# Two products for three: 512 and 256 moving columns in the second SwiGLU's gate and up and in the SSD output projection

## Chip, core and metric

One core of a Trainium2 chip runs the whole program. The metric is device time in microseconds (us); the kernel before takes 2457.24 us (median of 3 runs, 2456.81 to 2458.86).

## What is computed

An encoder trunk of two layers on 256 tokens plus 16 learned meta tokens (272 in all), width 2048, in fp32. Layer 0 mixes tokens with a grouped 2-D Fourier transform, layer 1 with a bidirectional Mamba-2 (SSD) mixer; each mixer is followed by a dense SwiGLU of hidden width 5632. Cut to the two places that the change touches:

```python
def swiglu_ffn(u, w_gate, w_up, w_down):
    return (jax.nn.silu(u @ w_gate) * (u @ w_up)) @ w_down

def bidir_ssd_mixer(u, w_in, ...):
    ...
    return gated_group_rms_norm(y, z, norm_w) @ w_out      # y: 272 x 4096, w_out: 4096 x 2048

for i in range(2):
    h = h + (fourier_mixer, bidir_ssd_mixer)[i](rms_norm(h, norm_mix_w[i]), ...)
    h = h + swiglu_ffn(rms_norm(h, norm_ffn_w[i]), w_gate[i], w_up[i], w_down[i])
return rms_norm(h, norm_final_w)[:, 16:]                   # the meta tokens are dropped at the end
```

Since the meta tokens are dropped, the last output projection and the last SwiGLU need only the 256 other tokens.

## The kernel before

**Split operands.** Every large product is made of fp32 numbers split in two fp32r parts, high and low. `mm3` (L102 to L106) issues three matmuls into one accumulator: high weights by high activation (L104), high weights by low activation (L105), low weights by high activation (L106). Here the weights are stationary (128 x 128, loaded anew for each matmul) and the activation moves: 272 columns where all tokens are needed, 256 where the meta tokens are not (`lo` = NM = 16). The third low-by-low product is left out everywhere.

**Weights.** `weights` (L84) takes 1 MB units by DMA on SP into three buffers; ACT casts each half to the high part `wh` (L97), DVE subtracts it from the original for the low part `wl` (L98), four buffers of each. A part is 128 x 1024 and serves 24 matmuls here (four feature blocks by two accumulators in gate and up, two feature blocks by four accumulators in the output projection).

**Products and accumulators.** `gemm_in` (L115) makes two blocks of 128 output features at a time, over 16 feature blocks `k`, alternating between two accumulators. Accumulators (`mmtile`, tag mm) are PSUM tiles of 128 x 512 fp32, four of them in rotation, so a pair can start when the pair before the last has been read out.

**Gate and up of the last SwiGLU** (`swiglu`, L360, with `lo` = 16): per pair of hidden blocks the gate product, then DVE multiplies the accumulator with 1/rms (`rbc`, L375), ACT takes the silu (L377), POOL multiplies with 1/rms once more (L378); then the up product, which DVE multiplies with that (L383), ACT rounds to `hh` (L384), POOL makes `hl` (L385). 88 such products run in all (44 blocks, gate and up), each of 16 `k`, 1408 calls of `mm3`. After each piece of the hidden layer the down product of the piece before it runs (`down1`, L787), with 512 moving columns.

**SSD output projection** (`out_group`, L557): for a group of 512 channels and a quarter `q` of the output features, two pairs (`jp`) of accumulators; a pair takes four `k` by two accumulators by `mm3`, 24 matmuls of 256 columns. DVE adds the accumulator to the residual `hT` (L567). There are eight groups, eight pairs each, 64 pairs, 512 calls of `mm3`. Groups 0 to 6 run inside the SSD stage, two steps behind the group whose inputs are computed, in between other small products of that stage (states L605 to L613, the mixing L626 to L642). The last group runs alone at the end of the stage, and each finished block of the residual there goes through `norm_block` (L142): ACT writes `gh` (L144) and a square, DVE writes `gl` (L145), POOL adds up the squares. These blocks are the operands of the first gate product.

**What sets the order.** Past the Fourier stage the program is put in order by the tile framework's scheduler, engine by engine, by its own estimates; weight parts are raised in priority (L96). Every engine then runs its list strictly in that order, and waits where an operand or a buffer isn't ready.

## Time and profile before

| | |
|---|---|
| runs | 2456.81, 2457.24, 2458.86 us; median 2457.24 |
| profiled execution, first to last instruction | 2455.8 us |
| profiled execution, own time | none is given beside its span; the median of the runs lies 1.4 us above the span |
| PE busy | 2428.0 us (99%), 17958 matmuls |
| DVE busy | 1484.5 us (60%) |
| ACT busy | 1214.1 us (49%) |
| TensorE clock granted | 0.998 of full speed |
| DMA | 438.66 MB, mean 179 GB/s |

How to read it: an engine's busy time is the union of its instructions' spans. A matmul's recorded span overlaps that of the next, so the time that a stream of them costs is the distance between starts (length of a stretch over the number of matmuls in it), not the mean duration. A wait is told with the instruction that ended it.

### The profile page before, as it was taken

The numbers are of one execution on the slowest core, as the hardware profiler recorded it, in microseconds if no ns is written. First come the engines' busy times: TensorE is split into PE (matmuls) and PEld (weight loads), VectorE is DVE, ScalarE is ACT, GpSimd is POOL, SyncE is SP. The second block draws the span as 40 slices with busy tenths as digits, with TensorE's granted clock in tenths as the row PEclk, the third lists the DMA queues.
The fourth block names the chain that finished last, engine by engine and source line by source line (L and its number), as shares of the span: only waits on it lengthen the run. The fifth ranks groups of instructions, "written<-read, shape, count | busy, mean of one in ns | idle before, by whom it ended". The sixth has DMA issues, their size and how long they took to land.

```text
span 2455.8 us, 42928 instructions
## 1 busy us (share of the span) xinstructions
PE 2428.0 (99%) x17958; PEld 2316.9 (94%) x17958; DVE 1484.5 (60%) x2020; ACT 1214.1 (49%) x1784; POOL 406.6 (17%) x361
## 2 busy tenths in 40 slices
PE   8999999999999999999999999999999999999998
PEld 8999999999999999888989989989999998989887
DVE  7564545545454568778668668668554555555556
ACT  6444333343434346878557558445444343444434
POOL 3111111010101112232221221112211010102000
PEclk9999999999999999999999999999999999999999
DMA  5555555555555555655455555454555555555553
GB/s 164 175 178 179 173 173 176 181 175 172 175 181 177 172 173 175 213 175 186 164 179 193 177 172 184 159 172 157 201 187 178 189 189 189 189 190 188 189 192 134
DMA packets 115506, 438.66 MB, mean 179 GB/s; under 512 B 7360, under 2 KB 8080, under 8 KB 115136
## 3 DMA queue, kind: packets, MB, share of 16 engines
q1 hardware_dynamic: 110336, 417.86, 50.4%
q0 software_dynamic: 4832, 17.99, 2.3%
q8 instruction: 141, 2.31, 0.4%
q14 instruction: 53, 0.43, 0.0%
q10 hardware_dynamic: 144, 0.07, 0.0%
HBM read 433.66 MB, written 2.23 MB: 177 GB/s over the span
## 4 chain that ended last, share of the span: by engine, by line
PE 89%; DVE 3%; DMA 3%; issue 2%; ACT 2%; POOL 1%; SPq 0%; DVEq 0%; ACTq 0%; POOLq 0%
PE mm L105 29%; PE mm L106 28%; PE mm L104 28%; DMA pb<-scr 2%; DVE wl L98 1%; PE tp L642 1%; ACT wh L97 1%; DVE ca L544 1%; PE tp L626 0%; PE tp L665 0%; DMA w<-fnet_w_out 0%; POOL pb L701 0%; ACT pb L584 0%; DMA x<-x 0%; PE tp L608 0%
## 5 line engine op out<-in xcount | busy, mean ns | idle before, releaser
L98 DVE TENSOR_TENSOR wl<-w,wh 128x1024 fp32r<-128x1024 f32 x786 | 970.0, 1236 | 840.7 <-ACT wh L97 832.7
L97 ACT CAST wh<-w 128x1024 fp32r<-128x1024 f32 x786 | 822.8, 1048 | 1096.6 <-PE mm L105 809.2
L105 PE MATMUL mm<-gl,wh 128*128 128x272 f32 (+2 forms) x3600 | 1026.0, 285 | 0.0
L106 PE MATMUL mm<-gh,wl 128*128 128x272 f32 (+2 forms) x3600 | 1022.3, 284 | 0.5 <-DVE wl L98 0.5
L104 PE MATMUL mm<-gh,wh 128*128 128x272 f32 (+2 forms) x3600 | 1022.4, 284 | 0.1
L104 PEld LDWEIGHTS mm<-gh,wh 128*128 128x128 f32 x3600 | 678.2, 188 | 1.1 <-issue 0.5
L106 PEld LDWEIGHTS mm<-gh,wl 128*128 128x128 f32 x3600 | 676.3, 188 | 0.9 <-DVE wl L98 0.7
L105 PEld LDWEIGHTS mm<-gl,wh 128*128 128x128 f32 x3600 | 676.1, 188 | 0.8 <-issue 0.5
L378 POOL TENSOR_TENSOR s<-s,rbc 128x272 f32<-128x272 f32 (+1 forms) x88 | 96.4, 1113 | 816.4 <-ACT s L377 816.4
L105 PE MATMUL mm<-hl,wh 128*128 128x272 f32 x704 | 203.7, 289 | 0.0
L106 PE MATMUL mm<-hh,wl 128*128 128x272 f32 x704 | 202.7, 288 | 0.0
L104 PE MATMUL mm<-hh,wh 128*128 128x272 f32 x704 | 200.9, 285 | 0.0
L385 POOL TENSOR_TENSOR hl<-t,hh 128x272 fp32r<-128x272 f32 (+1 forms) x88 | 97.0, 1121 | 397.1 <-ACT hh L384 397.1
L104 PE MATMUL mm<-yh,wh 128*128 128x256 f32 x512 | 146.5, 288 | 3.8 <-DVE hT L567 3.3
L105 PE MATMUL mm<-yl,wh 128*128 128x256 f32 x512 | 143.6, 281 | 0.5 <-DVE yl L671 0.5
L106 PE MATMUL mm<-yh,wl 128*128 128x256 f32 x512 | 143.5, 281 | 0.0
L105 PE MATMUL mm<-wl,hh 128*128 128x512 f32 x352 | 137.1, 390 | 0.0
L104 PE MATMUL mm<-wh,hh 128*128 128x512 f32 x352 | 137.0, 389 | 0.0
L106 PE MATMUL mm<-wh,hl 128*128 128x512 f32 x352 | 137.0, 389 | 0.0
L104 PEld LDWEIGHTS mm<-hh,wh 128*128 128x128 f32 x704 | 132.9, 189 | 0.0
L106 PEld LDWEIGHTS mm<-hh,wl 128*128 128x128 f32 x704 | 132.3, 188 | 0.0
L105 PEld LDWEIGHTS mm<-hl,wh 128*128 128x128 f32 x704 | 132.1, 188 | 0.0
(279 smaller groups left out, 2858.5 us busy)
## 6 DMA issues: line engine op xcount, KB each, us to landing
w<-ffn_w_gate SPq DMA_DIRECT2D x88, 1024.0 KB, 5.1
w<-ffn_w_up SPq DMA_DIRECT2D x88, 1024.0 KB, 5.1
w<-w_down SPq DMA_DIRECT2D x80, 1024.0 KB, 5.1
w<-w_xbc SPq DMA_DIRECT2D x48, 1024.0 KB, 5.2
w<-w_z SPq DMA_DIRECT2D x32, 1024.0 KB, 5.3
w<-ssd_w_out SPq DMA_DIRECT2D x32, 1024.0 KB, 5.1
w<-fnet_w_out SPq DMA_DIRECT2D x16, 1024.0 KB, 5.1
pb<-scr POOLq DMA_DIRECT2D x32, 512.0 KB, 5.6
```

What stands on the lines that cost most here:

```text
L97: SC.copy(wh, w[:, ks, :])
L98: V.tensor_tensor(out=wl, in0=w[:, ks, :], in1=wh.bitcast(F32), op=ALU.subtract)
L104: PE.matmul(ps, lhs[0], rhs[0], start=start, stop=False)
L105: PE.matmul(ps, lhs[0], rhs[1], start=False, stop=False)
L106: PE.matmul(ps, lhs[1], rhs[0], start=False, stop=stop)
L378: GP.tensor_tensor(out=s1, in0=s1, in1=rbc[:, lo:], op=ALU.mult)
L385: GP.tensor_tensor(out=hl[:, f, :], in0=t2, in1=hh[:, f, :].bitcast(F32), op=ALU.subtract)
L544: V.scalar_tensor_tensor(out=a[:, o0:o1], in0=u[:, i0 : i0 + o1 - o0], scalar=w(j), in1=a[:, o0:o1], op0=ALU.mult, op1=ALU.add)
L642: PE.matmul(py[:, e * HD : (e + 1) * HD], kern[c][:, e, :], xt[:, c, e * HD : (e + 1) * HD], start=True, stop=True)
```

## The change

The high and the low part of the moving activation stand next to each other for each feature block, 256 + 256 columns. `mm3t` takes the place of `mm3` in the two places: one matmul of the high weights over all 512 columns, which leaves high-by-high in the first half of the accumulator and high-by-low in the second; then one of the low weights over the first 256 columns, added to the first half. The halves are added when the accumulator is read: in the SwiGLU ACT copies the second half to SBUF and DVE adds the first (`halves`), then the old multiplication follows from SBUF; in the output projection DVE adds both halves to the residual one after the other. For this `gh` and `gl` become two views of one buffer `g2`, and `gt`, a third view that lies over them, holds the pairs for the last SwiGLU; `yh` and `yl` become halves of one tile `yt`. The second matmul closes the accumulation. (The diff also drops comments, which is left out here.)

```diff
-    gh = const.tile([P, NB, L], F32R, name="gh")
-    gl = const.tile([P, NB, L], F32R, name="gl")
+    g2 = const.tile([P, 2 * NB * L], F32R, name="g2")
+    gh, gl = (g2[:, i * NB * L : (i + 1) * NB * L].rearrange("p (b t) -> p b t", t=L) for i in range(2))
+
+    gt = g2[:, : NB * 2 * S].rearrange("p (b t) -> p b t", t=2 * S)
...
+    def mm3t(ps, lhs, twin, start, stop):
+
+        PE.matmul(ps, lhs[0], twin, start=start, stop=False)
+        PE.matmul(ps[:, :S], lhs[1], twin[:, :S], start=False, stop=stop)
+
+    def halves(out, ps):
+        SC.copy(out, ps[:, S:])
+        V.tensor_tensor(out=out, in0=ps[:, :S], in1=out, op=ALU.add)
...
                 for j in range(2):
-                    mm3(pss[j][:, :n], wsl(u, k, j * P), gsl(k0 + k, lo), k0 + k == 0, k0 + k == NB - 1)
+                    if lo == NM:
+                        mm3t(pss[j], wsl(u, k, j * P), gt[:, k0 + k, :], k0 + k == 0, k0 + k == NB - 1)
+                    else:
+                        mm3(pss[j][:, :n], wsl(u, k, j * P), gsl(k0 + k, lo), k0 + k == 0, k0 + k == NB - 1)
...
-        SC.activation(gh[:, b, lo:], hT[:, b, lo:], AF.Identity, bias=0.0, scale=wcol)
-        V.scalar_tensor_tensor(out=gl[:, b, lo:], in0=hT[:, b, lo:], scalar=wcol,
-                               in1=gh[:, b, lo:].bitcast(F32), op0=ALU.mult, op1=ALU.subtract)
+
+        high, low = (gt[:, b, :S], gt[:, b, S:]) if lo == NM else gsl(b, lo)
+        SC.activation(high, hT[:, b, lo:], AF.Identity, bias=0.0, scale=wcol)
+        V.scalar_tensor_tensor(out=low, in0=hT[:, b, lo:], scalar=wcol,
+                               in1=high.bitcast(F32), op0=ALU.mult, op1=ALU.subtract)
...
-                    V.tensor_tensor(out=t1, in0=ps[:, :n], in1=rbc[:, lo:], op=ALU.mult)
+                    if lo == NM:
+                        halves(t1, ps)
+                    V.tensor_tensor(out=t1, in0=t1 if lo == NM else ps[:, :n], in1=rbc[:, lo:], op=ALU.mult)
...
-                    V.tensor_tensor(out=t2, in0=ps[:, :n], in1=s2[j], op=ALU.mult)
+                    if lo == NM:
+                        halves(t2, ps)
+                    V.tensor_tensor(out=t2, in0=t2 if lo == NM else ps[:, :n], in1=s2[j], op=ALU.mult)
...
-                        mm3(pss[j][:, :S], wsl(u, k, (2 * jp + j) * P), (yh[:, k, :], yl[:, k, :]), k == 0, k == 3)
+                        mm3t(pss[j], wsl(u, k, (2 * jp + j) * P), yt[:, k, :], k == 0, k == 3)
...
-                    V.tensor_tensor(out=hT[:, m, NM:], in0=ps[:, :S], in1=hT[:, m, NM:], op=ALU.add)
+                    for half in (ps[:, :S], ps[:, S:]):
+                        V.tensor_tensor(out=hT[:, m, NM:], in0=half, in1=hT[:, m, NM:], op=ALU.add)
...
-            yh = sp.tile([P, 4, S], F32R, tag="yh", name="yh", bufs=2)
-            yl = sp.tile([P, 4, S], F32R, tag="yl", name="yl", bufs=2)
+            yt = sp.tile([P, 4, 2 * S], F32R, tag="yt", name="yt", bufs=2)
+            yh, yl = yt[:, :, :S], yt[:, :, S:]
```

The scheduler places the new instructions, and moves others. Up to the first output projection the lists of all engines are the same but for names. Three places follow; a name's number tells its buffer apart, and the new program numbers its lines and buffers anew (L587 there is L567 here, L100 is L98, L691 is L671, L160 is L145, L631 is L611).

DVE in the first out group (channels group 0): pairs of accumulators mm_12510/12511, mm_12538/12539, mm_12576/12577 before. Before:

```order
L567 TENSOR_TENSOR hT_69<-mm_12510,hT_69 128x256
L567 TENSOR_TENSOR hT_69<-mm_12511,hT_69 128x256
L671 SCALAR_TENSOR_TENSOR yl_11525<-tp_12435,cols_74,yh_11524 128x128
L671 SCALAR_TENSOR_TENSOR yl_11525<-tp_12448,cols_74,yh_11524 128x128
L567 TENSOR_TENSOR hT_69<-mm_12538,hT_69 128x256
L671 SCALAR_TENSOR_TENSOR yl_11525<-tp_12435,cols_74,yh_11524 128x128
L671 SCALAR_TENSOR_TENSOR yl_11525<-tp_12448,cols_74,yh_11524 128x128
L567 TENSOR_TENSOR hT_69<-mm_12539,hT_69 128x256
L98 TENSOR_TENSOR wl_12663<-w_12660,wh_12662 128x1024
L98 TENSOR_TENSOR wl_12667<-w_12660,wh_12666 128x1024
L567 TENSOR_TENSOR hT_69<-mm_12576,hT_69 128x256
```

Now, from the second pair (mm_12528/12529) on, with the third (mm_12560/12561) and fourth (mm_12582/12583):

```order
L587 TENSOR_TENSOR hT_69<-mm_12528,hT_69 128x256
L100 TENSOR_TENSOR wl_12635<-w_12632,wh_12634 128x1024
L587 TENSOR_TENSOR hT_69<-mm_12528,hT_69 128x256
L100 TENSOR_TENSOR wl_12639<-w_12632,wh_12638 128x1024
L587 TENSOR_TENSOR hT_69<-mm_12529,hT_69 128x256
L587 TENSOR_TENSOR hT_69<-mm_12560,hT_69 128x256
L587 TENSOR_TENSOR hT_69<-mm_12529,hT_69 128x256
L587 TENSOR_TENSOR hT_69<-mm_12560,hT_69 128x256
L587 TENSOR_TENSOR hT_69<-mm_12561,hT_69 128x256
L587 TENSOR_TENSOR hT_69<-mm_12582,hT_69 128x256
L587 TENSOR_TENSOR hT_69<-mm_12561,hT_69 128x256
```

Each accumulator is now read twice. The two weight parts come between the reads of the second pair, and the second read of mm_12529 stands behind the first read of mm_12560, an accumulator that PE finishes later.

PE at the fourth pair of the same group. Before, its matmuls alternated between the two accumulators and the state products (L605 to L613) stood behind the pair. Now:

```order
L117 MATMUL mm_12582<-yt_10956,wl_12553 128x256
L116 MATMUL mm_12582<-yt_10956,wh_12556 128x512
L117 MATMUL mm_12582<-yt_10956,wl_12557 128x256
L116 MATMUL mm_12582<-yt_10956,wh_12556 128x512
L117 MATMUL mm_12582<-yt_10956,wl_12557 128x256
L628 MATMUL tp_12607<-xw_12458,btok_11558 128x512
L116 MATMUL mm_12583<-yt_10956,wh_12552 128x512
L117 MATMUL mm_12583<-yt_10956,wl_12553 128x256
```

The first accumulator is completed, then a state product, then the second is begun. A group's first state product (xwM) moves up in the same way, ahead of the third pair.

DVE in the last out group, four of whose pairs are mm_17826/17827, mm_17858/17859, mm_17900/17901 and mm_17932/17933. Before (pairs mm_18183/18184, mm_18221/18222, mm_18269/18270), the reads stood two by two:

```order
L567 TENSOR_TENSOR hT_69<-mm_18183,hT_69 128x256
L567 TENSOR_TENSOR hT_69<-mm_18184,hT_69 128x256
L145 SCALAR_TENSOR_TENSOR gl_71<-hT_69,cols_74,gh_70 128x256 x2
L567 TENSOR_TENSOR hT_69<-mm_18221,hT_69 128x256
L567 TENSOR_TENSOR hT_69<-mm_18222,hT_69 128x256
L98 TENSOR_TENSOR wl_18348<-w_18345,wh_18347 128x1024
L145 SCALAR_TENSOR_TENSOR gl_71<-hT_69,cols_74,gh_70 128x256 x2
L567 TENSOR_TENSOR hT_69<-mm_18269,hT_69 128x256
L98 TENSOR_TENSOR wl_18352<-w_18345,wh_18351 128x1024
```

Now:

```order
L587 TENSOR_TENSOR hT_69<-mm_17858,hT_69 128x256
L160 SCALAR_TENSOR_TENSOR g2_70<-hT_69,cols_73,g2_70 128x256
L100 TENSOR_TENSOR wl_17967<-w_17964,wh_17966 128x1024
L160 SCALAR_TENSOR_TENSOR g2_70<-hT_69,cols_73,g2_70 128x256
L587 TENSOR_TENSOR hT_69<-mm_17858,hT_69 128x256
L100 TENSOR_TENSOR wl_17971<-w_17964,wh_17970 128x1024
L160 SCALAR_TENSOR_TENSOR g2_70<-hT_69,cols_73,g2_70 128x256
L587 TENSOR_TENSOR hT_69<-mm_17859,hT_69 128x256
L587 TENSOR_TENSOR hT_69<-mm_17900,hT_69 128x256
L587 TENSOR_TENSOR hT_69<-mm_17859,hT_69 128x256
```

The reads of a pair are spread: two weight parts and three low parts of the norm stand between the first and the last read of mm_17858/17859.

## Rows read from the trace of the kernel before

**Rows 1.** The page: engines' busy time, the granted clock in 40 slices, the chain.
```profile
PE 2428.0 (99%) x17958; PEld 2316.9 (94%) x17958; DVE 1484.5 (60%) x2020; ACT 1214.1 (49%) x1784; POOL 406.6 (17%) x361
...
PEclk9999999999999999999999999999999999999999
...
PE 89%; DVE 3%; DMA 3%; issue 2%; ACT 2%; POOL 1%; SPq 0%; DVEq 0%; ACTq 0%; POOLq 0%
```

**Rows 2.** Busy time by stretch: gate and up, down, z, five out stretches.
```profile
core 0: us, PE busy (x) PEld busy (x) DVE busy (x) ACT busy (x) POOL busy (x), PEclk, DMA share, GB/s
1934.00:2023.84 89.84, 89.84 (x769) 89.84 (x768) 45.68 (x49) 37.99 (x46) 15.19 (x14) 1.00 0.57 189
2023.85:2067.40 43.55, 43.55 (x194) 36.05 (x193) 24.08 (x25) 17.48 (x18) 2.18 (x2) 1.00 0.56 192
1137.56:1159.87 22.31, 22.31 (x99) 18.09 (x97) 17.72 (x22) 19.80 (x33) 0.91 (x1) 1.00 0.55 195
1652.68:1664.11 11.43, 11.43 (x98) 11.43 (x98) 7.12 (x13) 3.67 (x5) 2.33 (x2) 1.00 0.41 132
1162.24:1176.24 14.00, 14.00 (x105) 12.40 (x104) 11.12 (x21) 11.29 (x22) 6.71 (x6) 1.00 0.57 202
1176.25:1190.25 14.00, 14.00 (x108) 12.80 (x106) 7.91 (x14) 4.79 (x5) 1.16 (x1) 1.00 0.46 153
1680.52:1706.31 25.79, 23.80 (x192) 23.01 (x193) 22.16 (x40) 17.39 (x37) 11.90 (x11) 1.00 0.37 127
```

**Rows 3.** Timeline of PE where the down product ends and gate begins: start, duration.
```profile
2067.19 0.39 PE L106 MATMUL mm<-wh,hl 128*128 128x512 f32 x1
2067.41 0.28 PE L104 MATMUL mm<-gh,wh 128*128 128x256 f32 x1
2067.53 0.28 PE L105 MATMUL mm<-gl,wh 128*128 128x256 f32 x1
```

**Rows 4.** Groups by shape, PE: line, operation, shapes, count | busy us, mean ns.
```profile
L104 PE MATMUL mm<-gh,wh 128*128 128x256 f32 x1408 | 394.5, 280 | 0.1
...
L104 PE MATMUL mm<-yh,wh 128*128 128x256 f32 x512 | 146.5, 288 | 3.8 <-DVE hT L567 3.3 <-ACT yh L670 0.5
```

**Rows 5.** Groups by shape, DVE and ACT: the operations nearest to the added ones.
```profile
L567 DVE TENSOR_TENSOR hT<-mm,hT 128x256 f32<-128x256 f32 x128 | 48.9, 416 | 9.2 <-PE mm L106 9.1
...
L383 DVE TENSOR_TENSOR t<-mm,s 128x256 f32<-128x256 f32 x44 | 17.1, 425 | 7.0 <-PE mm L106 6.1 <-POOL s L378 0.9
```

**Rows 6.** Groups by shape, ACT: a copy of 256 columns from PSUM.
```profile
L554 ACT COPY xt<-tp 128x256 f32<-128x256 f32 x32 | 11.6, 362 | 0.2 <-PE tp L553 0.2
```

**Rows 7.** Timeline of the first out group from 1162.24: DVE's reads, PE's state product.
```profile
1165.99 0.74 DVE L567 TENSOR_TENSOR hT<-mm,hT 128x256 f32<-128x256 f32 x2
1166.66 0.59 DVE L671 SCALAR_TENSOR_TENSOR yl<-tp,cols,yh 128x128 fp32r<-128x128 f32 x2
...
1173.78 1.12 PE L605 MATMUL tp<-xwM,btokM 16*128 16x512 f32 x2
```

**Rows 8.** Waits of PE from 1000 to 1706: us in total, times, longest.
```profile
PE mm L104 <- DVE hT L567: 3.3, 4, 1.6
```

**Rows 9.** Groups of DVE from 1680.5 to 1713.3, the last out group and its tail.
```profile
L98 DVE TENSOR_TENSOR wl<-w,wh 128x1024 fp32r<-128x1024 f32 x10 | 12.2, 1216 | 1.3 <-ACT wh L97 1.2
L145 DVE SCALAR_TENSOR_TENSOR gl<-hT,cols,gh 128x256 fp32r<-128x256 f32 x16 | 10.9, 702 | 0.9 <-ACT gh L144 0.9
L567 DVE TENSOR_TENSOR hT<-mm,hT 128x256 f32<-128x256 f32 x16 | 6.1, 413 | 0.7 <-PE mm L106 0.6
L671 DVE SCALAR_TENSOR_TENSOR yl<-tp,cols,yh 128x128 fp32r<-128x128 f32 x7 | 2.2, 345 | 0.8 <-ACT yh L670 0.8
```

**Rows 10.** Timeline of DVE after the last out group: last add, last low part.
```profile
1710.87 0.41 DVE L567 TENSOR_TENSOR hT<-mm,hT 128x256 f32<-128x256 f32 x1
...
1712.34 0.95 DVE L145 SCALAR_TENSOR_TENSOR gl<-hT,cols,gh 128x256 fp32r<-128x256 f32 x1
```

More of the change, by code (lines that the diff above doesn't have):

```diff
@@ L555, in to_tokens, with out_group @@
             SC.copy(dstM, ps[:NM, 2 * P : 3 * P])
-        def out_group(gi, q, yh, yl):
+        def out_group(gi, q, yt):
             u = weights(w_out, gi * 4, 4, q * 512, 512)
@@ L683, in group_rest @@
             later(4, norm)
-            return yh, yl
+            return yt
         def decays(gi):
@@ L764, in encoder @@
                         for q in (2 * h2, 2 * h2 + 1):
-                            out_group(go, q, *outs[go])
+                            out_group(go, q, outs[go])
                             if go == G - 2 and h2 == 1:
@@ L772, in encoder @@
         for q in range(4):
-            out_group(G - 1, q, *outs[G - 1])
+            out_group(G - 1, q, outs[G - 1])
     with ExitStack() as fx:
```

## The prediction, as made before the changed kernel ran

> **What bounds the kernel now.** I read the page first: PE is busy 99% of the span at full granted clock in all 40 slices, and 89% of the chain that ended last is PE [rows 1]. So time is won only where PE issues less or faster, and lost where PE is made to wait. Second, busy time by stretch, to get PE's price for a matmul: a stream of matmuls costs the distance between starts, so a stretch's length over its count. Gate and up of the last SwiGLU: 768 matmuls of 256 columns start in 89.84 us, 117.0 ns each. The down product: 192 of 512 columns in 43.55 us, 226.8 ns. The z product of the SSD stage, also 512 columns: 96 in 22.31 us, 232.4 ns. An undisturbed half group of the output projection: 96 of 256 columns in 11.43 us, 119.1 ns, the first start included [rows 2]. The timeline shows the same step by step where 512 columns give way to 256: 0.22, then 0.12 us [rows 3]. Third, the waits: over the SSD stage PE's largest wait for DVE's residual adds is 3.3 us in four times [rows 8], and nearly all of what its matmuls waited for in the out groups is that add [rows 4]. DVE is the second engine to watch: 45.68 of 89.84 us in gate and up, but 11.12 of 14.00 us in the first half of an out group, and 22.16 of 25.79 in the last group [rows 2].
>
> **The part that is removed.** A call of `mm3` was three matmuls of 256 columns, now it is one of 512 and one of 256: the same 768 columns, one weight load and one start fewer. By the distances: gate and up 3 x 117.0 = 351.0 ns before; out groups 3 x 119.1 = 357.3. Afterwards one 512 and one 256. No row shows the two in turn, so I bound the pair. The dear end is 232.4 + 119.1 = 351.5, with the z row; the cheap end 226.8 + 113.4 = 340.2, if the 256 columns go at the down product's price per column (half of 226.8). I take 226.8 + 119.1 = 345.9: the down product is nearest, because its moving and stationary operands lie in the same even steps as those of `gt` and `yt` with the weight parts do, while in z the stationary part steps by 272 columns; and 119.1 is the even-step price of 256 columns. That gives, with 1408 calls in gate and up and 448 in out groups 0 to 6 [rows 4]:
>
> - gate and up: 1408 x (351.0 - 345.9) = 1408 x 5.1 ns = 7.2 us (ends: 0.7 lost, 15.2 won);
> - out groups 0 to 6: 448 x (357.3 - 345.9) = 448 x 11.4 ns = 5.1 us (ends: 2.6 and 7.7).
>
> So 12.3 us less (ends 1.9 and 22.9). The last group's 64 calls are left out here, since DVE sets its pace (below).
>
> From 226.8 and 119.1 the rows make a start cost 11.4 ns beside its columns (2 x 119.1 - 226.8). The Trainium skill (TensorE: Matmul & The Clock Gate, Back-to-back issue gap) gives a matmul of N columns N / 2.4 + 2.5 ns at full clock; by it a start fewer saves 2.5 ns, and 1856 calls save an estimated 4.6 us, which speaks against most of this gain. By it the two prices would be an estimated 216 and 109 ns; the trace has 226.8 and 117.0 to 119.1, so the two differ, and the sum goes by the rows.
>
> **What is added in gate and up: nothing on the path.** 88 ACT copies at about 0.36 us [rows 6] and 88 DVE adds at about 0.42 us [rows 5], with the old multiplication reading SBUF. A pair of products lasts 32 calls x 0.346 = 11.1 us on PE; in this time DVE gets 2 x 0.42 = 0.85 us and ACT 0.72 us more. DVE there is half idle, ACT more so [rows 2]. The accumulators of a pair are wanted again a whole pair later, 11.1 us, and the copy, the add and the multiplication take under 3 us. Without that cover it would be 88 x 0.8 = 70 us, so it's the four accumulators that carry it. The first pair even frees its accumulators sooner than before, as the add needs no 1/rms. At the end of the kernel the last piece's `hh` and `hl` come about 0.8 us later; the down product of the piece before them, 48 matmuls at 226.8 ns or 10.9 us, runs meanwhile.
>
> **What is added in out groups 0 to 6.** 16 DVE adds of 0.416 us more in each [rows 5], 6.7 us in some 28 us, where DVE is busy 11.12 + 7.91 us of 28.00 [rows 2]: room overall, 25.7 of 28, but the first half comes to 11.12 + 3.33 = 14.45 us in a half that PE would pass in 13.6 (14.00 less 32 x 11.4 ns). Behind an add wait the next weight parts on DVE, and for the add waits the pair after the next, whose accumulators it frees. I walked through the first group along the new order, with the durations of the rows. Pair 1 starts at 1162.24 and a pair lasts 8 x 0.346 = 2.77 us. The reads of pair 1 start at 1165.99, as now; four adds and two `yl` in between end near 1168.1. Pair 3 starts at 1167.8 plus the state product that now stands ahead of it, 1.12 us [rows 7]: no wait. Pair 2's first accumulator is free near 1170.6, behind one weight part of 1.2 us [rows 9]; its second near 1173.0, behind the second weight part and the first read of pair 3. Pair 4 begins with the first accumulator at 1171.7, and the state product fills the time up to the second: no wait either. The moved state products thus absorb the delay. I put 2 us on all seven groups, for the one in which DVE was already late (the longest wait of 1.6 us [rows 8]) and small rests elsewhere; ends 0 and 17 us.
>
> **What is added in the last out group.** From 1680.5 to 1713.3 DVE did 12.2 + 10.9 + 6.1 + 2.2 = 31.4 us of work in 32.8 us [rows 9]. Sixteen more adds at 0.413 are 6.6 us, 38.0 in all, so this work ends 5.2 us later than now, near 1718 instead of 1713.3 [rows 10]. PE's own work would be shorter, but its pairs wait for accumulators, and the weight parts for the next stage (ten in the stretch) stand in the same list. Walking the order as above, PE starts the gate product some 5 us later than at 1706.3. I take 5 us; ends 2 (weight parts get ahead of the reads in time) and 7.
>
> **Sum.** -12.3 + 2 + 5 = -5.3 us against the profiled execution, whose span is 2455.8: 2450.5. The median of the runs lies 1.4 us above that span, so I forecast **2451.9 us**. 0.2% is 4.9 us: about what a measurement of this kernel can tell from no change; faster means under 2452.3, slower over 2462.2.
>
> **Rivals.**
>
> 1. *All adds are covered.* Then 12.3 us and the last group's own 64 x 11.4 ns = 0.7 are won: 2457.2 - 13.0 = 2444.2. For it: PE waited so little for DVE until now [rows 8]. Against: DVE has 1.4 us left in the last group's 32.8 [rows 9]. 0.17.
> 2. *Time goes with the columns alone.* The 512-column matmul then takes the z stretch's 232.4 ns in company with the 256: gate and up lose 0.7, out groups win 2.6, and with the 2 + 5 of waits the time is 2457.2 - 1.9 + 7 = 2462.3, at the edge of slower. For it: 512 columns did take 232.4 where the product stood in the SSD stage [rows 2], and the first distance after a change of size is not settled. Against: 44 us of down product at 226.8. 0.20. By the 2.5 ns a start of the Trainium skill (same page and section) the time would be an estimated 2457.2 - 4.6 + 7 = 2459.6.
> 3. *DVE sets the pace of every out group.* A pair's two accumulators are free 0.83 us later each time; if that reaches PE in three pairs of each of the seven groups, 7 x 3 x 0.8 = 16.8 us instead of 2: 2457.2 - 12.3 + 16.8 + 5 = 2466.7, slower. It decides where the last of a pair's four adds ends after the start of the pair after the next. For it: the second read of a pair now stands behind a read that waits for a later pair, and DVE has 14.45 us of work in a half of 13.6. Against: the walk above finds the state products in the right places. 0.18.
>
> **How the numbers follow.** The forecast has 0.45, its own range 2446 to 2458 by the pair's price (2 ns a call is 3.7 us) and 2 to 3 us on the last group. Range over the cases: from 2441, which holds rival 1 and a cheaper pair, to 2464, which holds rival 2; most of rival 3 is left out. Faster: rival 1 and six tenths of the forecast, 0.44. Slower: nearly all of rival 3 and under half of rival 2, 0.24. Same: 0.32.
>
> **What would show it.** In gate and up, pairs of starts of about 227 and 119 ns, so a piece of eight blocks in 88.5 us instead of 89.84; 233 and 119 there is rival 2. PE's waits for `hT` are 2 us or less before the last group and 4 to 6 us in it, with the first gate matmul about 5 us later relative to the group's start; waits of 2 us in each group are rival 3, none in the last group rival 1. DVE x216 and ACT x88 more, PE x1920 fewer. I'd be wrong altogether if the 512 and 256 in turn cost under 340 or over 352 ns, or if PE waited in gate and up.

## The result and the profile after

| | before | after |
|---|---|---|
| median of the runs | 2457.02 us (2455.92 to 2458.86, 4 runs) | 2475.2 us (2474.3 to 2478.73, 4 runs) |
| profiled execution, first to last instruction | 2455.8 us | 2473.3 us (its own time 2475.11) |
| ratio of the runs | | 1.0076, 95% interval 1.0064 to 1.0088 |

The change makes the kernel 18.7 us slower (0.0076 x 2457; interval 15.7 to 21.6). Below, a ratio is turned into us over the kernel before in the same way, since every batch of runs had runs of the kernel before beside it. The forecast was 2451.9 us, its range ended at 2464: the time lies outside, and the sign is wrong.

The page of the kernel after answers to [rows 1]: 1920 matmuls fewer, 216 DVE and 88 ACT instructions more, as foreseen, but PE is busy for 2.6 us more, and its share of the chain fell from 89% to 84%.

```profile
PE 2430.6 (98%) x16038; PEld 2233.0 (90%) x16038; DVE 1563.5 (63%) x2236; ACT 1236.3 (50%) x1872; POOL 415.1 (17%) x361
...
PE 84%; DVE 6%; issue 3%; ACT 3%; DMA 3%; POOL 1%; SPq 0%; DVEq 0%; ACTq 0%; POOLq 0%
```

Where the time went is read by stretch. I cut both executions at the same three matmuls: the first of out group 0, the first of out group 5 (from there groups 5 to 7 follow one another), and gate's first. The kernel before, in the columns of [rows 2]:

```profile
1162.24:1623.49 461.25, 457.73 (x3179) 418.29 (x3178) 329.09 (x530) 286.34 (x499) 88.20 (x71) 1.00 0.52 177
1623.49:1706.31 82.82, 80.37 (x639) 76.10 (x638) 63.94 (x120) 39.75 (x70) 20.33 (x18) 1.00 0.41 142
```

The kernel after: a piece of eight blocks in gate and up, the down product behind it, then the same two stretches, and three places inside the second of them.

```profile
1950.98:2040.85 89.87, 89.87 (x513) 78.77 (x512) 51.87 (x62) 41.88 (x61) 18.37 (x14) 1.00 0.56 189
2040.85:2084.41 43.56, 43.56 (x195) 36.05 (x193) 25.04 (x27) 17.91 (x20) 2.67 (x2) 1.00 0.56 190
1162.38:1629.90 467.52, 459.86 (x2859) 403.48 (x2858) 354.48 (x610) 284.17 (x499) 80.15 (x71) 1.00 0.51 174
1629.90:1723.21 93.31, 81.79 (x447) 67.78 (x446) 80.01 (x167) 40.24 (x71) 17.70 (x18) 0.98 0.39 133
1684.60:1689.42 4.82, 0.00 (x1) 0.00 (x1) 4.77 (x16) 1.03 (x1) 0.00 (x0) 1.00 0.62 210
1689.42:1692.48 3.06, 3.06 (x15) 3.06 (x16) 0.41 (x2) 0.73 (x2) 0.00 (x0) 0.56 0.74 238
1693.87:1723.21 29.34, 23.69 (x128) 19.62 (x129) 26.22 (x51) 17.01 (x36) 9.98 (x11) 1.00 0.29 98
```

Three things are to be seen. Gate and up gained nothing: 89.87 us for the piece that took 89.84 [rows 2], so 89.87 / 256 = 351.0 ns a pair. The stretch of groups 0 to 4, with the products between them, is 6.3 us longer, and the stretch of groups 5 to 7 is 10.5 us longer. Inside this last one stand 4.82 us in which PE starts nothing while DVE is busy for 4.77, then 3.06 us at a granted clock of 0.56 (mostly the 1.2 GHz level), and a last group of 29.34 us instead of 25.79 [rows 2]. From gate's first matmul to the last matmul both kernels take 738.1 us.

The waits of PE over the SSD stage answer to [rows 8]. The adds' 3.3 us became 8.6 (2.9 in group 3, 5.6 in the last group), and there is a new wait of 4.8 us, for `dg`, which no add writes:

```profile
PE mm L116 <- DVE hT L587: 8.6, 6, 2.9
PE tp L685 <- DVE dg L680: 4.8, 1, 4.8
PE mm L107 <- DVE wl L100: 2.6, 3, 1.4
PE mm L116 <- DVE yt L691: 1.0, 1, 1.0
PE tp L570 <- DVE yt L691: 0.8, 2, 0.5
PE tp L625 <- POOL xwM L621: 0.7, 1, 0.7
PE tp L570 <- ACT xs L565: 0.5, 1, 0.5
```

`dg` is the diagonal of 1/rms by which a group's gated output is scaled on its way back to feature-major. In the last group it ends a row of twelve DVE operations on two columns (`sums`, then the eleven of `rsqrt`). DVE's timeline of the kernel before, from `sums` to `dg`, takes 5.3 us, with four adds and two weight parts in between:

```profile
1671.32 0.17 DVE L654 TENSOR_SCALAR sums<-sums 128x2 f32<-128x2 f32 x1 [0.52 <-ACT sqj L647]
...
1672.39 0.74 DVE L567 TENSOR_TENSOR hT<-mm,hT 128x256 f32<-128x256 f32 x2
...
1676.65 0.43 DVE L660 TENSOR_TENSOR dg<-ident,rgy 128x256 f32<-128x256 f32 x1
```

In the kernel after it takes 8.4 us, with nine adds and four weight parts:

```profile
1680.58 0.17 DVE L674 TENSOR_SCALAR sums<-sums 128x2 f32<-128x2 f32 x1 [0.51 <-ACT sqj L667]
1680.65 1.22 DVE L100 TENSOR_TENSOR wl<-w,wh 128x1024 fp32r<-128x1024 f32 x1
1681.79 0.42 DVE L587 TENSOR_TENSOR hT<-mm,hT 128x256 f32<-128x256 f32 x1
...
1684.53 0.15 DVE L151 SCALAR_TENSOR_TENSOR rgy<-rgt,rgy 128x2 f32<-128x2 f32 x1
1684.60 0.42 DVE L587 TENSOR_TENSOR hT<-mm,hT 128x256 f32<-128x256 f32 x1
1684.93 0.15 DVE L149 TENSOR_TENSOR rgt<-rgy 128x2 f32<-128x2 f32 x1
...
1687.82 1.22 DVE L100 TENSOR_TENSOR wl<-w,wh 128x1024 fp32r<-128x1024 f32 x1
1688.95 0.42 DVE L680 TENSOR_TENSOR dg<-ident,rgy 128x256 f32<-128x256 f32 x1
```

An add stands between almost every two operations of the chain, and DVE idles nowhere in it. PE's timeline shows what waits: group 6's last matmul starts at 1684.33, and the next thing in PE's order needs `dg`.

```profile
1684.33 0.28 PE L117 MATMUL mm<-yt,wl 128*128 128x256 f32 x1
1689.42 3.48 PE L685 MATMUL tp<-dg,yg 128*128 128x128 f32 x16 [4.82 <-DVE dg L680]
1693.87 0.50 PE L116 MATMUL mm<-yt,wh 128*128 128x512 f32 x1 [0.97 <-DVE yt L691]
```

Before, `dg` was ready near 1677.1 and PE came for it at 1678.1: one microsecond of slack. The stage ahead had shifted by 6.4 us, but `dg` came 12.3 us later (1676.65 to 1688.95): 2.9 us because `sums` came later still, 3.0 us because the chain got longer. The row of operations ahead of `sums`, the last group's second mixing, got longer in the same way. From its first operation on DVE to `sums` it took 5.6 us, with two adds and one weight part in between, and takes 10.6 us, with eleven adds and two weight parts. Its start before and after:

```profile
1665.72 0.68 DVE L627 TENSOR_TENSOR yg<-tp,tm 128x512 f32<-128x512 f32 x1
1670.02 0.69 DVE L647 TENSOR_TENSOR yg<-tp,tm 128x512 f32<-128x512 f32 x1
```

From group 6's first matmul to the last group's, the kernel before takes 27.84 us and the kernel after 34.62, so 6.8 more: the wait of 4.8, 1.4 for the products with `dg` at the lower clock (3.06 us instead of 1.67), and 0.5 in the wait for `yt` behind them.

```profile
1652.68:1680.52 27.84, 27.38 (x228) 26.71 (x228) 21.33 (x46) 10.22 (x15) 2.33 (x2) 1.00 0.44 152
1659.25:1693.87 34.62, 28.84 (x164) 24.97 (x163) 28.22 (x68) 11.28 (x18) 2.34 (x2) 0.95 0.45 152
```

### The profile page after: what moved, and what is told of

It is laid out like the page before. It is cut to its first block, busy times and chain, and to the rows that moved or that the text cites. A ratio compares the mean times of both kernels' runs of the same rounds, so it can differ in the third digit from the quotient of the medians.

```text
span 2473.3 us, 39469 instructions
## 1 busy us (share of the span) xinstructions
PE 2430.6 (98%) x16038; PEld 2233.0 (90%) x16038; DVE 1563.5 (63%) x2236; ACT 1236.3 (50%) x1872; POOL 415.1 (17%) x361
## 4 chain that ended last, share of the span: by engine, by line
PE 84%; DVE 6%; issue 3%; ACT 3%; DMA 3%; POOL 1%; SPq 0%; DVEq 0%; ACTq 0%; POOLq 0%
PE mm L107 18%; PE mm L108 18%; PE mm L106 18%; PE mm L116 17%; PE mm L117 9%; DMA pb<-scr 2%; DVE wl L100 2%; DVE ca L563 1%; ACT wh L99 1%; ACT pb L604 1%; PE tp L662 1%; DMA w<-fnet_w_out 0%; PE tp L646 0%; DVE pb L606 0%; DVE hT L587 0%
## 5 line engine op out<-in xcount | busy, mean ns | idle before, releaser
L100 DVE TENSOR_TENSOR wl<-w,wh 128x1024 fp32r<-128x1024 f32 x786 | 973.3, 1241 | 759.7 <-ACT wh L99 757.4
L107 PE MATMUL mm<-g,wh 128*128 128x272 f32 (+1 forms) x2192 | 633.7, 289 | 0.0
L108 PE MATMUL mm<-g,wl 128*128 128x272 f32 (+1 forms) x2192 | 630.8, 288 | 0.5 <-DVE wl L100 0.5
L106 PE MATMUL mm<-g,wh 128*128 128x272 f32 (+1 forms) x2192 | 628.2, 287 | 0.0
L116 PE MATMUL mm<-g,wh 128*128 128x512 f32 x1408 | 494.7, 394 | 0.0
L106 PEld LDWEIGHTS mm<-g,wh 128*128 128x128 f32 x2192 | 414.0, 189 | 0.6 <-issue 0.2
L108 PEld LDWEIGHTS mm<-g,wl 128*128 128x128 f32 x2192 | 411.9, 188 | 0.9 <-DVE wl L100 0.7
L107 PEld LDWEIGHTS mm<-g,wh 128*128 128x128 f32 x2192 | 411.8, 188 | 0.5 <-issue 0.5
L117 PE MATMUL mm<-g,wl 128*128 128x256 f32 x1408 | 398.2, 283 | 0.0
L116 PEld LDWEIGHTS mm<-g,wh 128*128 128x128 f32 x1408 | 264.5, 188 | 60.9
L117 PEld LDWEIGHTS mm<-g,wl 128*128 128x128 f32 x1408 | 265.0, 188 | 0.2
L395 POOL TENSOR_TENSOR s<-s,rbc 128x272 f32<-128x272 f32 (+1 forms) x88 | 105.3, 1206 | 808.6 <-ACT s L394 808.6
L116 PE MATMUL mm<-yt,wh 128*128 128x512 f32 x512 | 189.5, 412 | 9.9 <-DVE hT L587 8.6
L404 POOL TENSOR_TENSOR hl<-t,hh 128x272 fp32r<-128x272 f32 (+1 forms) x88 | 107.4, 1230 | 388.5 <-ACT hh L403 388.5
L117 PE MATMUL mm<-yt,wl 128*128 128x256 f32 x512 | 142.1, 282 | 0.0
```

What stands on the lines that cost most here:

```text
L100: V.tensor_tensor(out=wl, in0=w[:, ks, :], in1=wh.bitcast(F32), op=ALU.subtract)
L106: PE.matmul(ps, lhs[0], rhs[0], start=start, stop=False)
L107: PE.matmul(ps, lhs[0], rhs[1], start=False, stop=False)
L108: PE.matmul(ps, lhs[1], rhs[0], start=False, stop=stop)
L116: PE.matmul(ps, lhs[0], twin, start=start, stop=False)
L117: PE.matmul(ps[:, :S], lhs[1], twin[:, :S], start=False, stop=stop)
```

## The experiments

Theory A, formed from these rows: the pair of 512 and 256 costs what the three matmuls of 256 cost, so there is nothing to win, and all of the loss comes from the added `hT` adds in the SSD stage, a large part of it from group 6's, which hold up the last group's norm. The rivals are told with each run.

**Each half of the change alone.** First gate and up changed, the output projection as before:

```diff
-                        mm3t(pss[j], wsl(u, k, (2 * jp + j) * P), yt[:, k, :], k == 0, k == 3)
+                        mm3(pss[j][:, :S], wsl(u, k, (2 * jp + j) * P), (yt[:, k, :S], yt[:, k, S:]), k == 0, k == 3)
...
-                    for half in (ps[:, :S], ps[:, S:]):
+                    for half in (ps[:, :S],):
```

> Only the second SwiGLU's gate and up have the matmul of 512 columns and their halves added; the SSD output projection is as before. Theory A (the time of a pair goes with its 768 columns, 351.6 ns in the trace after against 351.2 ns for the three before, and the whole loss lies ahead of gate and up): within 1.5 us of the kernel before, say 0 to +1.5. Rival B (the pair does save 5 ns of 351, and the trace after hides it behind something that the output projection leaves behind): 1408 pairs give 7 us, so -7. Rival C (the loss is that of gate and up, the shift ahead of them only a delay that would be caught up): about +17.

Measured: 1.0002 (0.9992 to 1.0011), +0.5 us. A and not B: no gain was hidden. Then the output projection alone, where gate and up keep `mm3` and read the accumulator as before:

```diff
-                    if lo == NM:
+                    if False:
                         mm3t(pss[j], wsl(u, k, j * P), gt[:, k0 + k, :], k0 + k == 0, k0 + k == NB - 1)
...
```

> Only the SSD output projection has the matmul of 512 columns and two adds a block; gate and up are as before. Theory A: the whole loss is here, +16 to +18.5 over the kernel before, and the start of gate stands 16.8 us later as in the trace after. Rival C: within 2 us of the kernel before. Either way the sum of this and of the run with gate and up alone tells whether the two halves of the change touch each other: theory A has them add up to +18 within 1.5 us.

Measured: 1.0072 (1.0059 to 1.0085), +17.7 us. The two add up to 18.2 of the 18.7 us. Within the intervals they do not touch each other, and the loss is the output projection's.

**The adds or the form of the matmuls.** The output projection alone again. Once with the pair, but a single add:

```diff
-                    for half in (ps[:, :S], ps[:, S:]):
+                    for half in (ps[:, :S],):
```

> Gate and up as before; in all eight SSD output groups the matmuls of 512 and 256 columns as changed, but one hT add a block instead of two: the high-low products are summed and left out of the result. Theory A (the adds and the place they take in VectorE's order are what costs; the pair itself costs what the three matmuls cost): -1 to +4 over the kernel before, the wait for dg under 1 us, the waits for hT in the last group under 2 us in sum. Rival F (the form of the matmuls costs, by state products that now stand inside pairs and by longer waits for an accumulator of 512 columns): +10 or more.

And once with two adds, but matmuls of the old size:

```diff
-                        mm3t(pss[j], wsl(u, k, (2 * jp + j) * P), yt[:, k, :], k == 0, k == 3)
+                        w = wsl(u, k, (2 * jp + j) * P)
+                        PE.matmul(pss[j][:, :S], w[0], yt[:, k, :S], start=k == 0, stop=False)
+                        PE.matmul(pss[j][:, S:], w[0], yt[:, k, S:], start=False, stop=False)
+                        PE.matmul(pss[j][:, :S], w[1], yt[:, k, :S], start=False, stop=k == 3)
```

> Gate and up as before; in all eight SSD output groups three matmuls of 256 columns as before the change, but the high-low one into the other half of the accumulator, so that two hT adds a block are needed as in the change. Theory A: the loss is there with matmuls of the old size, +13 to +19 over the kernel before, with a wait of 3 to 5 us for dg. Rival F: within 4 us of the kernel before.

Measured: one add 1.0011 (1.0002 to 1.0020), +2.7 us; two adds with old matmuls 1.0054 (1.0040 to 1.0067), +13.3 us. With one add, by stretch:

```profile
1163.09:1625.34 462.25, 457.98 (x2859) 402.22 (x2858) 328.18 (x530) 285.91 (x499) 86.64 (x71) 1.00 0.51 176
1625.34:1708.07 82.73, 79.64 (x447) 66.47 (x446) 64.84 (x121) 39.93 (x72) 18.72 (x18) 1.00 0.42 146
```

With two adds and matmuls of 256 columns:

```profile
1163.38:1629.09 465.71, 460.76 (x3180) 420.50 (x3178) 354.23 (x610) 285.14 (x499) 86.89 (x71) 0.99 0.52 175
1629.09:1723.89 94.80, 85.23 (x640) 80.25 (x638) 78.39 (x166) 41.69 (x72) 20.94 (x19) 0.95 0.37 123
```

The stretch of groups 5 to 7 has its old length with one add (82.73 against 82.82) and is 12 us longer with two, though the matmuls have the old size. (The profiled execution with two adds is the slowest of its five, 2475.14 us against a median of 2472.3, and its granted clock in this stretch is 0.95; the median is 13.3 us over the kernel before.) The wait for `dg` is there in the second and not in the first:

```profile
PE tp L688 <- DVE dg L683: 4.4, 1, 4.4
```

So A against F for the larger part of the loss. It is not shown that the form costs nothing: by the runs it is worth 2.7 us with one add and 4.4 with two (17.7 less 13.3), both with intervals that begin near nothing. In the stretches it shows as 1.0 us in groups 0 to 4 with one add; two executions of one and the same order, those of the kernel before and of gate and up alone, differ there by 1.4 us (461.25 and 459.83).

**Which group's adds.** The whole change, with only the last group's output projection put back, and then with those of groups 6 and 7 (`gi >= G - 2` in its place):

```diff
-                        mm3t(pss[j], wsl(u, k, (2 * jp + j) * P), yt[:, k, :], k == 0, k == 3)
+                        if gi == G - 1:
+                            mm3(pss[j][:, :S], wsl(u, k, (2 * jp + j) * P), (yt[:, k, :S], yt[:, k, S:]), k == 0, k == 3)
+                        else:
+                            mm3t(pss[j], wsl(u, k, (2 * jp + j) * P), yt[:, k, :], k == 0, k == 3)
...
-                    for half in (ps[:, :S], ps[:, S:]):
+                    for half in (ps[:, :S], ps[:, S:])[: 1 if gi == G - 1 else 2]:
```

> The changed kernel, with the last SSD group's output projection done as before, in three matmuls of 256 and one add a block; groups 0 to 6 are as changed. Theory A (the last group's own double adds cost some 4.7 us in waits of TensorE for hT, while the wait for dg comes from group 6's adds and stays): 4 to 6 us faster than the changed kernel, the wait for dg still 3 to 5 us. Rival D (VectorE's whole load around the last group sets it): over 9 us faster, and the wait for dg gone too. Rival E (the waits for hT before the last group's end were hidden ones, the last group being bound by its weights' parts): within 2 us of the changed kernel.

> The changed kernel, with the output projection of groups 6 and 7 in three matmuls of 256 and one add a block as before, groups 0 to 5 as changed. Theory A (the wait of 4.8 us for dg and the low clock behind it come from group 6's second adds, which stand ahead of the norm's small operations; the waits for hT from group 7's): the stretch from group 6 to gate is back at its length before, and what is left over the kernel before is +6 to +9, from groups 0 to 5. Rival M (the wait for dg comes from what groups 0 to 5 left behind, such as a later mixing): the wait for dg is still over 3 us and the time +11 to +13.

Measured: without the last group 1.0053 (1.0041 to 1.0066), +13.0 us, so its part of the change is worth 5.6 us, and the wait for `dg` stays:

```profile
PE tp L688 <- DVE dg L683: 4.8, 1, 4.8
PE mm L116 <- DVE hT L590: 2.9, 1, 2.9
```

Without groups 6 and 7: 1.0016 (1.0007 to 1.0025), +3.9 us. The wait for `dg` is gone, and the stretch of groups 5 to 7 is back near its length before, 82.98 us against 82.82:

```profile
1161.40:1625.26 463.86, 459.14 (x2860) 403.55 (x2858) 355.32 (x610) 283.96 (x499) 81.04 (x71) 1.00 0.50 175
1625.26:1708.24 82.98, 80.45 (x575) 72.92 (x574) 69.96 (x136) 39.66 (x70) 19.62 (x18) 1.00 0.41 141
```

Group 6's part of the change is thus worth 9.1 us (13.0 - 3.9, numbers with intervals of 3 and 2 us to either side), though no matmul of group 6 waits for an add. The run puts back its second adds and its form together; that the wait for `dg` comes with the adds and not with the form is what the runs with one add and with two show. Group 6's own stretch holds 6.7 of the 9.1 us: it takes 34.53 us without the last group's part and 27.84, as before, without both. Another 2.7 us lie far ahead of it, from group 0 to group 1 (85.94 and 83.29 us), where both programs have the same order on every engine; why the one execution was slower there is not shown. What is left for groups 0 to 5, with gate and up, is 3.9 us, less than the 6 to 9 expected: in that number A was too high, since it rested on the 6.3 us that groups 0 to 4 lost in the kernel after.

**Only the order of the chain.** The whole change, with the last group's norm ahead of its time in DVE's list:

```diff
-            later(3, lambda: mix(1))
+            def mix1():
+                with tc.high_priority(offset=300) if gi == G - 1 else ExitStack():
+                    mix(1)
+
+            later(3, mix1)
...
-            later(4, norm)
+            later(3 if gi == G - 1 else 4, norm)
```

(and the same priority around `sums`, `rsqrt` and `dg`.)

> The changed kernel, with the last SSD group's second mixing and the small operations of its norm (rsqrt and the diagonal) put ahead of the hT adds of group 6 in VectorE's order, and nothing else; the number of adds is the same. Theory A (the norm's chain of 14 small operations waits in VectorE's queue behind adds that wait for TensorE's last products of group 6, so that TensorE finds nothing to do for 4.8 us and its clock is 0.56 in the 3 us after): 5 to 8 us faster than the changed kernel, that is +10 to +13 over the kernel before, no wait of over 1.5 us for dg, granted clock 1.00 there. Rival D (the adds themselves keep VectorE too busy, so that what the chain gains the adds lose, and the wait moves to hT): within 2 us of the changed kernel.

Measured: 1.0061 (1.0048 to 1.0073), +15.0 us, so 3.7 us faster than the changed kernel: less than the 5 to 8 expected, more than D's 2, though the two intervals overlap. The wait for `dg` is gone and the clock 1.00, and the stretch is 4.0 us shorter (89.31 against 93.31), but it holds a new wait, and the adds of the last group wait as before:

```profile
PE mm L116 <- DVE hT L587: 6.0, 6, 1.6
PE mm L116 <- DVE rgt L149: 2.2, 1, 2.2
```

In the order that came out, ten adds still alternate with the chain; it is the four weight parts that moved away. From group 5's first matmul to the last group's it takes 58.9 us, against 64.0 in the changed kernel and 57.0 before, so the order alone gives back 5.1 of 6.9 us there. The wait of 2.2 us is one of group 6's products, and the last group takes 1.1 us more than in the changed kernel. D has this much for it: DVE is busy for the same 80 us of groups 5 to 7 (80.06 and 80.01; 63.94 before), and no run shows an order that mends all of the loss. The trace also corrects a point of the expectation: the chain did not stand behind adds that wait for PE, since DVE idled nowhere; it stood behind adds and weight parts that take DVE's time.

**The price of the pair.** Why 351 ns, when 226.8 + 119.1 was to be had from the rows? The timeline of the kernel after, where the down product ends and gate begins, answers to [rows 3]:

```profile
2084.18 0.39 PE L108 MATMUL mm<-wh,hl 128*128 128x512 f32 x1
2084.41 0.40 PE L116 MATMUL mm<-g,wh 128*128 128x512 f32 x1
2084.64 0.27 PE L117 MATMUL mm<-g,wl 128*128 128x256 f32 x1
2084.75 0.39 PE L116 MATMUL mm<-g,wh 128*128 128x512 f32 x1
```

From start to start a 512 takes 0.23 us and a 256 some 0.12; over the trace from 1800 to 2100 the means are 230.8 and 120.3 ns. Eight runs bear on this. First the 512 by itself, in the kernel with gate and up alone changed:

```diff
-                        mm3t(pss[j], wsl(u, k, j * P), gt[:, k0 + k, :], k0 + k == 0, k0 + k == NB - 1)
+                        PE.matmul(pss[j], wsl(u, k, j * P)[0], gt[:, k0 + k, :], start=k0 + k == 0, stop=k0 + k == NB - 1)
```

> As the run with gate and up alone changed, without the matmul of 256 columns (the product of the weights' low parts with the activation's high ones is left out in gate and up). Prices the 512 by itself: theory A: 229 to 233 ns from start to start, as in the z products, which makes 1408 x (351 - 231) = 169 us less than before, some 2288 us. Rival G (the 512 alone is cheaper, 216 to 227 ns): 2267 to 2283 us.

Measured: 2294.36 us, 0.9334 (0.9317 to 0.9351), 6 us more than A's total. The piece of eight blocks:

```profile
1874.44:1934.16 59.72, 59.72 (x257) 48.06 (x256) 49.29 (x61) 41.13 (x60) 17.03 (x14) 1.00 0.82 264
```

59.72 / 256 = 233.3 ns for a 512 in gate, at the edge of A's 229 to 233, and 117.8 for the 256 that was left out (89.87 less 59.72). Per column that is 0.456 and 0.460 ns, and the three matmuls of before took 117.0 / 256 = 0.457. The down product's 0.443 (226.8 / 512, and 43.56 us here as before) is a price that gate does not get.

Then the order, two 512s and two 256s:

```diff
+                if lo == NM:
+                    ws = [wsl(u, k, j * P) for j in range(2)]
+                    for j in range(2):
+                        PE.matmul(pss[j], ws[j][0], gt[:, k0 + k, :], start=k0 + k == 0, stop=False)
+                    for j in range(2):
+                        PE.matmul(pss[j][:, :S], ws[j][1], gt[:, k0 + k, :S], start=False, stop=k0 + k == NB - 1)
...
```

> As the run with gate and up alone changed, but in the order 512, 512, 256, 256 over the two accumulators, so that sizes alternate half as often. Theory A (the time goes with the columns in any order): within 2 us of the kernel before and of that run. Rival G (the 231 ns after a 512 and the 120 after a 256 hold a price of changing size or of writing the same accumulator twice in a row): 5 ns of 351 a pair less, -7.

Measured: 0.9984 (0.9975 to 0.9993), -3.9 us.

```profile
1930.26:2019.44 89.18, 89.18 (x513) 78.04 (x512) 49.53 (x62) 41.74 (x60) 14.87 (x14) 1.00 0.55 190
```

348.4 ns a pair. The saving is more than A allowed; G has the direction and half the size. The next three were to tell what in the order does it: the old matmuls in that order (each of the three for both accumulators before the next), four and four, and four and four with two in a row into one accumulator.

```diff
-                    mm3(pss[j][:, :n], wsl(u, k, j * P), gsl(k0 + k, lo), k0 + k == 0, k0 + k == NB - 1)
+                g = gsl(k0 + k, lo)
+                for a, b in ((0, 0), (0, 1), (1, 0)) if lo == NM else ():
+                    for j in range(2):
+                        PE.matmul(pss[j][:, :n], wsl(u, k, j * P)[a], g[b], start=k0 + k == 0 and a + b == 0,
+                                  stop=k0 + k == NB - 1 and a == 1)
...
```

> The kernel before, its three matmuls of 256 kept, but in the second SwiGLU's gate and up each of the three is issued for both accumulators before the next (high-high twice, high-low twice, low-high twice). Tells whether the 4 us of the run with 512, 512, 256, 256 come from the order or from the size. Theory H (from the order: matmuls that follow one another into different accumulators cost 116 ns instead of 117 each): -3 to -5 against the kernel before. Theory I (from the size: only a 512 behind a 512 saves anything): within 1.5 us of the kernel before.

```diff
+                for kk in range(0, 8, 2):
+                    for k, j in ((kk + i // 2, i % 2) for i in range(4)):
+                        PE.matmul(pss[j], wsl(u, k, j * P)[0], gt[:, k0 + k, :], start=k0 + k == 0, stop=False)
+                    for k, j in ((kk + i // 2, i % 2) for i in range(4)):
+                        PE.matmul(pss[j][:, :S], wsl(u, k, j * P)[1], gt[:, k0 + k, :S], start=False,
+                                  stop=k0 + k == NB - 1)
...
```

> Gate and up alone changed, in the order of four matmuls of 512 and then four of 256, over two feature blocks and the two accumulators in turn. Theory I (a 512 behind a 512 into the other accumulator, 227.6 ns, and a 256 behind a 256, 116.3 ns, are the cheap ones, a 512 before a 256, 234.5 ns, the dear one): per pair some 229 + 117 = 346 ns, so -6 to -8 against the kernel before. Theory J (in a longer row of 512s the price goes up to the 229 and 237 ns of the run with 512s alone): 233 + 117 = 350, within 2 us of the kernel before.

The last of the three has `for j, k in ((i // 2, kk + i % 2) for i in range(4))` in both loops.

> As the run by fours, but two matmuls in a row go to the same accumulator (feature blocks k and k+1 of one output block, then of the other), so that each weight part is read in another stride and the activation changes with every matmul, as in the down products, whose 512s take 227 ns without exception. Theory K (what makes gate's 512s dear is that the same activation is read twice in a row, or the switch of accumulator): 227 + 117 = 344 ns a pair, -8 to -11 against the kernel before. Theory L (neither matters): the same as the run by fours within 1.5 us.

Measured: 1.0001 (0.9992 to 1.0010), 0.9999 (0.9990 to 1.0008) and 0.9999 (0.9990 to 1.0008). None saves anything: that speaks against H, against I in the run by fours, and against K. In the run by fours the piece takes

```profile
1932.48:2022.36 89.88, 89.88 (x513) 78.37 (x512) 49.53 (x62) 41.93 (x61) 14.87 (x14) 1.00 0.55 190
```

in which a 512 behind a 512 starts the next after 233.2 ns (J said 233), and a 256 after 117.7. Three more runs, on what was still open: the order by twos in the whole change, gate and up alone with the activation's tile at the pool's start, and the order by twos with the 256s begun at accumulator 1.

> The whole change, with gate and up in the order 512, 512, 256, 256 over the two accumulators. If the saving of the run with gate and up alone in this order belongs to the order, the stretch from gate's first matmul to the end is 734 to 735 us here too instead of 738.1, and the time is 3 to 5 us below the changed kernel's, still +13 to +15 over the kernel before, since the out groups' loss is not touched. If it belonged to that run alone: 738 us and no gain.

```diff
-    hT = const.tile([P, NB, L], F32, name="hT")
     g2 = const.tile([P, 2 * NB * L], F32R, name="g2")
...
+    hT = const.tile([P, NB, L], F32, name="hT")
     ident = const.tile([P, P], F32, name="ident")
```

> Gate and up alone changed, pairs in the change's order, with the tile that holds the activation put ahead of the residual in memory, so that it begins at the pool's start. Theory N (the place of the activation in memory makes gate's matmul of 512 columns dearer than the down products' 227 ns): 227 + 114 to 118 ns a pair, 5 to 10 us off the kernel before. Theory O (the place does not matter): 351 ns a pair, within 1.5 us of the kernel before.

```diff
-                    for j in range(2):
+                    for j in reversed(range(2)):
                         PE.matmul(pss[j][:, :S], ws[j][1], gt[:, k0 + k, :S], start=False, stop=k0 + k == NB - 1)
```

> Gate and up alone changed, in the order 512 and 512 over accumulators 0 and 1, then 256 and 256 over accumulators 1 and 0. Theory P (the saving comes with a switch of accumulator at every matmul): it goes, within 1.5 us of the kernel before. Theory Q (it comes with two matmuls of one size in a row, whatever their accumulators): -3 to -5 as in the run with accumulators 0 and 1 both times.

Measured: 1.0062 (1.0049 to 1.0074), +15.2 us and so 3.4 less than the change, with 734.3 us from gate's first matmul to the last; 0.9999 (0.9990 to 1.0008); 0.9983 (0.9974 to 0.9991), -4.2 us. The saving belongs to the order by twos (three runs of three), not to the accumulators (Q, not P), and the place of the activation in memory plays no part (O). Why two in a row are cheaper and four are not stays open, as does the down product's lower price.

The two runs by twos with the old output projection, at a median of 2453.33 us each, are faster than both kernels. That is 0.16 and 0.17% under the kernel before, less than the 0.2% that the prediction called no change, but both intervals lie wholly under 1.

## Why the prediction was wrong

By its own steps, in its order:

- **The pair at 345.9 ns in gate and up** (1408 calls, -7.2 us): wrong, and the first of two steps that failed. It measured 351.0, within 0.5 ns of the dear end of 351.5. I took the 512 from the down product, as the one with the most even steps, and z's 232.4 for the price of uneven ones. The runs show that it was the other way round: gate has even steps and pays z's price. Rival 2, time goes with the columns alone, is what happened in gate and up, with 0.20; it gave 0.7 us lost there, and the run with gate and up alone gave +0.5. Its sign, starts of 233 and 119 ns, is near what the trace shows (230.8 and 120.3). With it falls the start cost of 11.4 ns that I drew from the same two rows. The 2.5 ns of the Trainium skill (TensorE: Matmul & The Clock Gate, Back-to-back issue gap), which that section gives for a matmul by itself, would have been an estimated 1408 x 2.5 = 3.5 us. The runs show neither, since one start fewer per pair saved nothing: +0.5 us (-2.0 to +2.7).
- **Nothing on the path in gate and up**: right. PE waited for nothing there while DVE's busy time in the piece rose from 45.68 to 51.87 us, and the run with gate and up alone is at +0.5.
- **Out groups 0 to 6, 5.1 us won by the pair**: wrong by the same step; hardly anything of it came. In the half group from which I read 357.3 ns for three matmuls [rows 2], 24 calls in a row now take 8.44 us, 351.7 ns each with the first start, so half of what I counted. Over the whole of group 5, in which PE waits for nothing in either kernel and does the same other products, nothing is won (before and after):

```profile
1623.49:1652.68 29.19, 29.19 (x221) 26.38 (x220) 20.45 (x36) 12.14 (x19) 6.10 (x5) 1.00 0.43 145
1629.90:1659.25 29.35, 29.26 (x158) 23.19 (x156) 25.57 (x49) 11.96 (x19) 5.37 (x5) 1.00 0.42 144
```

With one add, where little else changed, the kernel was 2.7 us slower. That the moved state products absorb delays was right: group 3 aside, PE has no wait for `hT` in groups 0 to 6.

- **2 us of waits in out groups 0 to 6**: wrong, the second step that failed, in what it looked for. I asked where a matmul of the out groups waits for an accumulator. For groups 0 to 5 that was near: their waits, the place in group 3 at 2.9 us instead of 1.6 [rows 8], and what the adds push back in the stages between (weight parts, `yt`, `xs`) leave 3.9 us in all. Group 6 cost 9.1 us by the runs, 6.8 in its own stretch, and not one of its matmuls waited: its adds stood among the operations of the next group's mixing and norm, of which PE needs the last one. My walk followed the adds to the accumulators that they free and no further; it never asked which other results stand behind them in DVE's list, at the one place where PE has no other product left.
- **5 us in the last group**: right. Its stretch is 3.6 us longer, and without its part of the change the kernel is 5.6 us faster; PE's waits for `hT` in it are five, 5.6 us in sum.
- **Rival 3, DVE sets the pace of every out group**: it had the right time within 9 us and the right engine, but not the mechanism; there are no waits in each group.
- **The signs.** Neither sign of being wrong altogether came: the pair's 351.0 ns lie between 340 and 352, and PE waited for nothing in gate and up. The largest single loss stood at a place for which no sign was set.
- **The sum.** Between the runs the steps read +3.9 (groups 0 to 5, with the +0.5 of gate and up in it), +9.1 (group 6) and +5.6 (last group). They add up to the whole because each is the difference of two runs; the test of it is the two halves, 0.5 and 17.7, against 18.7.

## What to carry to other kernels

Putting two matmuls into one leaves their columns as they are; count columns first, and take a price per column from the product in question, not from the cheapest stretch of the trace. When work is added to an engine's list, follow every result behind it in that list to the one who waits for it, small operations above all, and look for the place where the waiting engine has nothing else: here work among a chain of twelve short operations, whose result had one microsecond of slack, was worth 7 to 9 of the 18.7 us. Work that does not stretch an average (DVE went from 60% to 63%) can still fill such a place.

## What the runs showed of the hardware

- The price per column of gate's matmuls is 0.457 ns whether they have 256 columns three times, 512 and 256 in turn, or four and four; only two and two goes down to 0.454 (89.18 / 256 / 768). The down product's 512 columns take 0.443 ns each in every run. What makes the difference is not shown.
- The wait for `dg` was paid twice. Behind its 4.82 us the granted clock was 0.56 for 3.06 us (row above), and the 16 matmuls there came 204 ns apart, where they took 111 at full clock. In group 3 the clock fell under 2 us after a wait of 2.92 us, to the lower level for 3 us; over the last group, with waits of up to 1.7 us, it is 1.00. The kernel after, group 3's wait and the stretch at the lower level:

```profile
1442.58:1445.78 3.20, 0.28 (x2) 0.03 (x1) 3.20 (x8) 1.81 (x6) 3.20 (x3) 1.00 0.22 55
1447.70:1450.70 3.00, 3.00 (x12) 2.62 (x11) 3.00 (x5) 0.00 (x0) 0.00 (x0) 0.50 0.14 57
```
